# One modulation's weight sums moved from TensorE to VectorE, in a two-block network on one core

## The chip, the cores and the metric

The kernel runs on one core of a Trainium2 chip. The metric is the device time of one execution in microseconds, as the median of several runs. Engines are called as the profile calls them: PE is TensorE (PEld its weight loads), DVE is VectorE, ACT is ScalarE, POOL is GpSimd and SP is the queue that issues most DMAs.

## The reference, cut to what matters

The first block has two layers (`i`) of two sublayers (`j`) each: a mixer and a mixture of experts. Every sublayer is modulated by three rows of 1024 numbers that come from one vector `c`:

```python
def adaln_params(c, w, b):
    m = jax.nn.silu(c) @ w + b                      # c: 1024, w: 1024 x 3072
    shift, scale, gate = jnp.split(m, 3, axis=-1)
    return shift[:, None, :], scale[:, None, :], gate[:, None, :]
...
for i in range(DEPTH):
    shift, scale, gate = adaln_params(c, ada_w[i, 0], ada_b[i, 0])
    h = x * (1.0 + scale) + shift
    y = stick_breaking_attention(h, ...) if i == 0 else retention(h, ...)
    x = layer_norm(DEEPNORM_ALPHA * x + (1.0 + gate) * y, ...)
    shift, scale, gate = adaln_params(c, ada_w[i, 1], ada_b[i, 1])
    h = x * (1.0 + scale) + shift
    y = grouped_moe(h, ...)
    x = layer_norm(DEEPNORM_ALPHA * x + (1.0 + gate) * y, ...)
```

A second block (a state-space branch, sparse attention and a large table of experts) follows; the change does not touch it.

## The kernel before, in words

Everything is fp32 and 256 tokens long. `block1` runs the four sublayers in order. Work that belongs to a later sublayer is written as generators in `net.jobs`; `background` (L106) advances the first of them by one step, and the stages call it between their own pieces: after each projection of the first attention (L454 to L459), four times after each group of heads (L473, `ATR` = 4), and after each piece of the output projection (L435).

`ada_all` (L230) is such a generator: for one sublayer it makes the three rows shift, scale and gate by `ada_rows` (L206), and after the second it turns shift and scale into columns (`ada_cols`, L240). `ada_rows` loads its slice of the weight, 1024 x 1024, in four steps of 1 MB (L217; two blocks of 128 rows each), so a step brings two blocks of 128 x 1024. In each step PE multiplies: the stationary operand is silu(c) of the block, repeated in 32 columns (`crep`), the moving one 256 columns of the weight; four such products land in four strips of 32 partitions of one PSUM tile `y` of the pool `acc` (four tiles in all), which is held over the four steps. DVE then copies it out (L228, or L226 with the bias for the gate). A weight tile is taken from the pool `w` or, during the attention (`WIDE` = 2), mostly from the pool `hl`; each has six tiles. The profile records each of these fp32 products as two matmul instructions, so a step of eight products stands there as 16.

The order of the jobs (L1685) is: what is left of sublayer (0, 0)'s modulation, the small parameters of the second block's state-space branch, the modulation of (0, 1), and shift and scale of (1, 0). By the calls that `background` gets, the first three weight steps of (0, 1) come between the last projections of the attention, the other nine after the first three groups of heads, and those of (1, 0) after the third and fourth.

The first attention (`stick`, L438) makes q, k and v for four groups of four heads by projections whose weights are split into a rounded part (ACT, L151) and a rest (DVE, L153). Then, group by group, `stick_keep` (L482) multiplies q and k into PSUM (two tiles `ps`, of four, and one `y` per group), and DVE makes two passes over each (L499, L500) into tiles `t` of the pool `t4` (six of 128 x 1024) and `t2`; ACT takes Exp (L505) and Ln (L512); DVE adds (L513); PE sums over keys (L514 to L518), ACT takes Exp again (L519, L521), PE multiplies by v (L526, L529), and the result is split (L151, L153). A group's second half (`stick_mix`) is written behind the first half of the next group. After that come the output projection (`proj_out`, whose weights go through `w` and `hl` as well), the layer norm, the router and the experts (`moe`), which load 1 MB tiles into `w`, `hl` and `a`, 16 of them ahead.

The written order is not the issue order: the framework's scheduler plans each engine's queue when the kernel is built, and moves an instruction forward where its engine would otherwise have nothing. On the chip each queue then runs in its planned order.

Of the kernel before, what the change touches and what calls it, by code (L numbers as in the profile page):

```python
# [8 lines left out]
F32 = mybir.dt.float32  # L9
# [6 lines left out]
OP = mybir.AluOpType  # L16
# [3 lines left out]
P = 128  # L20
# [3 lines left out]
KB = 8  # L24
# [21 lines left out]
SCORE = 4.16  # L46
PACE = 2.81
PK = 128

# [3 lines left out]
class Net:  # L55
# [142 lines left out]

    def ada_init(self):
        nc = self.nc  # L200
        sc = self.cst.tile([P, KB], F32, name="c_silu")
        nc.scalar.activation(sc, self.c_col, AF.Silu)
        self.crep = self.cst.tile([P, KB, 32], F32, name="c_rep")
        nc.vector.tensor_copy(self.crep, sc[:, :, None].to_broadcast([P, KB, 32]))

    def ada_rows(self, i, j, slot, out):  # L206

        nc = self.nc
        W = self.io["ada_w"][i, j].rearrange("(k p) n -> p k n", p=P)
        if slot == 2:  # L210
            bias = self.wk.tile([P, 256], F32, name="ada_b", bufs=1)
            nc.gpsimd.dma_start(bias, self.io["ada_gate_b"][i * 2 + j])
        pm = self.acc.tile([P, 512], F32, name="y")[:, :256]
        for k2 in range(4):
            w = self.hl(F32) if self.wide > k2 % 3 else self.w()
            w = w.rearrange("p (k n) -> p k n", k=2)
            nc.sync.dma_start(w, W[:, k2 * 2:k2 * 2 + 2, slot * D:(slot + 1) * D])  # L217
            for k in range(2):
                kk = k2 * 2 + k
                for c in range(4):  # L220
                    self.mm(pm[32 * c:32 * c + 32], self.crep[:, kk, :],
                            w[:, k, c * 256:(c + 1) * 256], kk == 0, kk == 7)
            if k2 < 3:
                yield
        if slot == 2:
            nc.vector.tensor_tensor(out, pm, bias, op=OP.add)  # L226
        else:
            nc.vector.tensor_copy(out, pm)  # L228
# [1226 lines left out]
    def gates(self, t, eT):  # L1455
# [3 lines left out]
        if t == 0:  # L1459
            buf = self.tk.tile([P, 2048], F32, name="s", bufs=2)  # L1460
            self.tmp.append(buf[:, :512])
            self.hot = buf[:, 512:].bitcast(F16).rearrange("p (r j n q) -> p r j n q", r=2, n=PK, q=4)

        def hots(t4):

            o2, oh, ol = (self.hot[:, t4 // 4 % 2, j] for j in range(3))
            of = lambda j: eT[:, j, None, t4:t4 + 4].to_broadcast([P, PK, 4])
            V.tensor_tensor(ol, self.iota4, of(0), op=OP.is_equal)
# [5 lines left out]
        def fill(t4, o2, oh, ol):  # L1474
# [6 lines left out]
            if n:  # L1481
                V.tensor_tensor(sl[:, :, :n], pg[:, :, :n], sl[:, :, :n], op=OP.mult)
            if n < PK:
                nc.scalar.copy(sl[:, :, n:], pg[:, :, n:])
# [10 lines left out]
    def peer(self, hn, big, out):  # L1495
# [5 lines left out]
        self.phase("U")  # L1501
        for i in range(0, PK, 2):
            ps = self.psum((P, 2, S))
# [25 lines left out]
        nc.gpsimd.dma_start(h, self.h_dram)  # L1529
        for i in range(PK):  # L1530
            vr = self.up.tile([P, D], F32, name="raw")
# [5 lines left out]
            for t in range(T):  # L1537
                ts = slice(t * P, t * P + P)
                for hf in range(2):
                    cs = slice(hf * 512, hf * 512 + 512)  # L1540
                    self.mm3(y[t][hf], (ah[:, ts], al[:, ts]), (vp[:, 0, cs], vp[:, 1, cs]), i == 0, i == PK - 1)
        for t in range(T):
# [282 lines left out]
```

## Time and profile before

| | before |
|---|---|
| median of 3 runs | 2111.67 us (2110.96 to 2115.21) |
| profiled execution | 2115.24 us |
| its span in the trace | 2113.5 us |
| PE busy | 1995.0 us, 94% |
| DVE busy | 1229.3 us, 58% |
| ACT busy | 788.1 us, 37% |
| DMA | 496.13 MB, 235 GB/s on the mean |

Busy times are sums over the span and hide that the stages have different limits. Starts are microseconds from the start of the span; a row of the timeline merges neighbouring instructions of one kind. The end of a matmul is modelled, so the time that one takes from PE is read from start to start.

### The profile page before, as it was taken

To read this page: it belongs to the slowest core of one execution; us is meant where nothing else is said; L and a number is where in the kernel's file an instruction comes from. 1 tells how busy PE (TensorE), PEld (TensorE's weight loads), DVE (VectorE), ACT (ScalarE), POOL (GpSimd) and SP (SyncE) were. 2 spreads that over 40 slices of the span, in tenths; PEclk is the share of its full clock that TensorE was granted. 3 is DMA by queue.
4 is the path that set the end of the run, shared out by engine and by line. 5 is a ranking of instruction groups with operands and counts; after the bars stand their busy time and mean duration, and the time that the engine had idled before them with its cause. 6 is when DMAs were issued, how large, how long until landed. Compare 5 with 4: busy or idle time off the path is not lost.

```text
span 2113.5 us, 32410 instructions
## 1 busy us (share of the span) xinstructions
PE 1995.0 (94%) x12822; PEld 1564.7 (74%) x12823; DVE 1229.3 (58%) x2491; ACT 788.1 (37%) x1232; POOL 461.5 (22%) x351
## 2 busy tenths in 40 slices
PE   6999999989999999997876899999999999999998
PEld 4967545438888844445764789899999998888886
DVE  3554211137885411114698559876999886555555
ACT  3353111124454211113323444555444444444444
POOL 1002000002331200000354133544666550000000
PEclk8998999999999899998998999999999999999999
DMA  9797799995775799995322261444554445555554
GB/s 389 293 399 273 262 395 391 395 379 208 285 289 175 258 362 393 395 393 216 129 82 99 96 246 51 150 150 142 167 191 160 140 150 189 189 190 189 190 189 150
DMA packets 155603, 496.13 MB, mean 235 GB/s; under 512 B 10145, under 2 KB 10561, under 8 KB 146865
## 3 DMA queue, kind: packets, MB, share of 16 engines
q1 hardware_dynamic: 152592, 483.42, 63.6%
q0 software_dynamic: 2848, 10.53, 1.3%
q8 instruction: 104, 1.70, 0.3%
q14 instruction: 59, 0.48, 0.1%
HBM read 486.30 MB, written 7.61 MB: 234 GB/s over the span
## 4 chain that ended last, share of the span: by engine, by line
PE 52%; DVE 10%; issue 2%; ACT 1%; POOL 1%; POOLq 0%; ACTq 0%; DVEq 0%
PE ps L163 27%; PE y L163 23%; DVE t L1157 1%; DVE pair L1510 1%; DVE et L1434 1%; PE y L1163 1%; DVE i L1411 1%; DVE hl L153 1%; DVE t L1158 1%; POOL hl L160 0%; DVE pos L1422 0%; DVE t L1153 0%; DVE t L1152 0%; DVE v L1410 0%; DVE big L1518 0%
## 5 line engine op out<-in xcount | busy, mean ns | idle before, releaser
L163 PE MATMUL ps<-hn,pair 128*128 128x256 f32 x3072 | 383.4, 285 | 4.5 <-DVE pair L1510 4.3
L163 PEld LDWEIGHTS ps<-hn,pair 128*128 128x128 f32 x3072 | 373.8, 191 | 5.6 <-DVE pair L1510 5.1
L1510 POOL TENSOR_TENSOR pair<-raw,pair 128x640 fp32r<-128x640 f32 x128 | 235.4, 1846 | 160.1 <-ACT pair L1508 148.8
L163 PE MATMUL ps<-w,t 128*64 128x512 f32 x576 | 254.6, 595 | 5.4 <-DVE t L194 3.8
L163 PE MATMUL ps<-hl,t 128*64 128x512 f32 x576 | 254.2, 595 | 0.0
L151 ACT CAST hl<-w 128x2048 fp32r<-128x2048 f32 x79 | 150.1, 1902 | 137.7 <-PE ps L163 66.4
L153 DVE TENSOR_TENSOR pair<-raw,pair 128x1024 fp32r<-128x1024 f32 x128 | 156.9, 1226 | 67.2 <-ACT pair L151 67.2
L163 PE MATMUL y<-pair,tmp 128*128 128x512 f32 x768 | 189.5, 395 | 0.0
L163 PE MATMUL y<-pair,eT 128*128 128x512 f32 x768 | 186.3, 391 | 0.0
L163 PEld LDWEIGHTS y<-pair,tmp 128*128 128x128 f32 x768 | 144.4, 188 | 33.9
L163 PEld LDWEIGHTS ps<-w,t 128*64 128x64 f32 x576 | 76.3, 137 | 125.2 <-issue 117.4
L163 PEld LDWEIGHTS y<-pair,eT 128*128 128x128 f32 x768 | 144.1, 188 | 32.5
L1508 ACT CAST pair<-raw 128x1024 fp32r<-128x1024 f32 x128 | 134.1, 1051 | 66.9 <-PE ps L163 23.9
L153 DVE TENSOR_TENSOR hl<-w,hl 128x2048 fp32r<-128x2048 f32 x51 | 120.3, 2360 | 46.6 <-ACT hl L151 43.5
L330 POOL TENSOR_TENSOR ln_st<-ln_st,c_mhalf 128x1 f32<-128x1 f32 x8 | 6.3, 792 | 600.4 <-ACT ln_st L327 600.4
L151 ACT CAST pair<-raw 128x1024 fp32r<-128x1024 f32 x128 | 133.8, 1046 | 1.1 <-issue 1.1
L711 DVE TENSOR_TENSOR t<-t,ps 128x512 f32<-128x512 f32 x16 | 11.0, 688 | 210.8 <-PE ps L163 210.8
L163 PE MATMUL ps<-hl,a 128*128 128x256 f32 x1008 | 130.2, 287 | 1.8 <-ACT hl L151 1.8
L163 PEld LDWEIGHTS ps<-hl,a 128*128 128x128 f32 x1008 | 124.0, 191 | 6.1 <-ACT hl L151 2.0
L163 PE MATMUL ps<-a,hl 128*128 128x256 f32 x864 | 107.4, 285 | 2.5 <-DVE a L153 1.3
L163 PEld LDWEIGHTS ps<-a,hl 128*128 128x128 f32 x864 | 105.2, 193 | 5.2 <-DVE a L153 1.5
L163 PEld LDWEIGHTS ps<-hl,t 128*64 128x64 f32 x576 | 74.5, 137 | 37.6 <-issue 37.1
(424 smaller groups left out, 3126.7 us busy)
## 6 DMA issues: line engine op xcount, KB each, us to landing
raw<-peer_u SPq DMA_DIRECT2D x128, 512.0 KB, 3.5
raw<-peer_v SPq DMA_DIRECT2D x128, 512.0 KB, 3.4
w<-ada_w SPq DMA_DIRECT2D x35, 1024.0 KB, 9.4
w<-moe_w_gate SPq DMA_DIRECT2D x24, 1024.0 KB, 16.1
w<-moe_w_up SPq DMA_DIRECT2D x24, 1024.0 KB, 14.1
w<-moe_w_down SPq DMA_DIRECT2D x24, 1024.0 KB, 14.0
hl<-moe_w_gate SPq DMA_DIRECT2D x24, 1024.0 KB, 14.3
hl<-moe_w_up SPq DMA_DIRECT2D x24, 1024.0 KB, 14.1
```

Source lines behind the costliest of these rows:

```text
L151: nc.scalar.copy(hi, src)
L153: nc.vector.tensor_tensor(lo, src, hi.bitcast(F32), op=OP.subtract)
L163: self.nc.tensor.matmul(out, lhsT=lhsT, rhs=rhs, start=start, stop=stop, skip_group_check=True)
L330: nc.gpsimd.tensor_tensor(st[:, 3:4], st[:, 2:3], self.mhalf[:, 0:1], op=OP.pow)
L711: nc.vector.tensor_tensor(hid, hid, pu, op=OP.mult)
L1157: V.tensor_tensor_scan(w[:, ri], d, a[:, ri], 0.0, op0=OP.mult, op1=OP.add)
L1158: V.tensor_tensor(a, w, bc(c), op=OP.mult)
L1163: self.nc.tensor.matmul(py[32 * q:32 * q + 32, :S], lhsT=self.s5_ct[ct][:, 4 * i + q], rhs=ab[q % 2][:, x, ri], start=j == 0, stop=j == 3, ...
L1411: V.max_index(ix[:, a, rs], v[:, a, rs], s)
L1434: V.tensor_reduce(et[:, 0:2, h], oh.rearrange("p a k j -> p a j k"), axis=AX.X, op=OP.add)
L1508: nc.scalar.copy(up[:, 0], ur)
L1510: lo = eng.tensor_tensor(up[:, 1, ks], ur[:, ks], up[:, 0, ks].bitcast(F32), op=OP.subtract)
```

## The change

For the sublayers in `SUMS`, here (0, 1) alone, `ada_rows` takes no PSUM tile over its four steps. It takes a tile `t4` of 128 x 1024 instead, and DVE multiplies each block of the weight by silu(c), one number per partition, and adds it to that tile: one `tensor_scalar` for the first block of a row and seven `scalar_tensor_tensor` for the others. After the last block PE sums over the partitions with a stationary operand of ones (four products into the four strips of a `y`), and the copy follows as before. Loads, their tiles and the steps stay as they are.

```diff
+SUMS = ((0, 1),)
...
-        sc = self.cst.tile([P, KB], F32, name="c_silu")
+        sc = self.csilu = self.cst.tile([P, KB], F32, name="c_silu")
...
-        pm = self.acc.tile([P, 512], F32, name="y")[:, :256]
+        rows = (i, j) in SUMS
+        acc = self.t4() if rows else None
+        pm = None if rows else self.acc.tile([P, 512], F32, name="y")[:, :256]
         for k2 in range(4):
...
             for k in range(2):
                 kk = k2 * 2 + k
+                if rows:
+
+                    ck = self.csilu[:, kk:kk + 1]
+                    if kk == 0:
+                        nc.vector.tensor_scalar(acc, w[:, k], ck, None, op0=OP.mult)
+                    else:
+                        nc.vector.scalar_tensor_tensor(acc, w[:, k], ck, acc, op0=OP.mult, op1=OP.add)
+                    continue
                 for c in range(4):
                     self.mm(pm[32 * c:32 * c + 32], self.crep[:, kk, :],
                             w[:, k, c * 256:(c + 1) * 256], kk == 0, kk == 7)
             if k2 < 3:
                 yield
+        if rows:
+            pm = self.acc.tile([P, 512], F32, name="y")[:, :256]
+            for c in range(4):
+                self.mm(pm[32 * c:32 * c + 32], self.ones[:, :32], acc[:, c * 256:(c + 1) * 256], True, True)
         if slot == 2:
```

## Rows read from the trace of the kernel before

**Rows 1.** The page: the span and the busy time of each engine

```profile
span 2113.5 us, 32410 instructions
PE 1995.0 (94%) x12822; PEld 1564.7 (74%) x12823; DVE 1229.3 (58%) x2491; ACT 788.1 (37%) x1232; POOL 461.5 (22%) x351
```

**Rows 2.** Busy time by stretch; columns in the first line

```profile
core 0: us, PE busy (x) PEld busy (x) DVE busy (x) ACT busy (x) POOL busy (x), PEclk, DMA share, GB/s
60.00:80.00 20.00, 20.00 (x175) 19.28 (x174) 13.36 (x18) 9.11 (x11) 0.55 (x1) 1.00 0.84 319
80.00:97.00 17.00, 17.00 (x169) 15.60 (x167) 11.83 (x21) 7.37 (x8) 0.54 (x1) 1.00 0.52 165
97.00:114.00 17.00, 17.00 (x146) 16.91 (x143) 4.87 (x6) 2.28 (x6) 1.08 (x2) 1.00 1.02 407
114.00:172.00 58.00, 57.33 (x489) 34.53 (x487) 36.65 (x64) 33.13 (x44) 2.18 (x4) 1.00 0.96 368
172.00:193.00 21.00, 21.00 (x96) 17.32 (x93) 5.94 (x8) 2.90 (x4) 0.00 (x0) 1.00 0.44 167
193.00:224.00 31.00, 27.75 (x143) 25.62 (x142) 13.49 (x55) 7.45 (x14) 12.21 (x12) 0.61 0.70 262
...
163.60:172.10 8.50, 8.50 (x45) 5.66 (x44) 6.11 (x18) 5.19 (x9) 0.00 (x0) 1.00 0.95 360
260.00:300.00 40.00, 40.00 (x226) 20.79 (x224) 7.81 (x19) 5.73 (x13) 0.00 (x0) 1.00 1.04 392
```

**Rows 3.** Timeline of PE from 94 to 172 us: start, duration, what

```profile
94.24 2.80 PE L163 MATMUL y<-w,c_rep 128*32 128x256 f32 x48
...
120.74 1.07 PE L163 MATMUL y<-hl,c_rep 128*32 128x256 f32 x16
121.74 0.70 PE L163 MATMUL ps<-t,c_nones 128*128 128x256 f32 x2
...
126.97 1.98 PE L163 MATMUL ps<-t,c_pack 128*128 128x512 f32 x4
...
134.25 1.13 PE L163 MATMUL ps<-a 128*128 128x256 f32 x4
...
172.11 21.15 PE L163 MATMUL y<-hl,a 128*128 128x512 f32 x92
```

**Rows 4.** Busy time of the instructions that read `c_rep`, 94 to 172 us

```profile
94.00:172.00 78.00, 21.59 (x320) 9.51 (x320) 0.00 (x0) 1.00 0.97 371
```

**Rows 5.** DVE on L316 and L335: ns min/median/max, first and last start

```profile
L316 DVE SCALAR_TENSOR_TENSOR a<-x_mid,a x8: 1217/1225/1227, 191.3 to 976.8; 128x1024 f32<-128x1024 f32 x8
...
L335 DVE TENSOR_SCALAR a<-a,ln_st x6: 812/813/1751, 195.7 to 714.5; 128x1024 f32<-128x1024 f32 x6
```

**Rows 6.** Timeline of SP from 60 us: issue of the loads

```profile
80.81 15.84 SPq L217 DMA_DIRECT2D w<-ada_w  x5
...
104.32 22.29 SPq L217 DMA_DIRECT2D hl<-ada_w  x9
...
148.97 1.89 SPq L671 DMA_DIRECT2D w<-moe_w_gate  x2
...
197.98 2.64 SPq L671 DMA_DIRECT2D a<-moe_w_gate  x1
...
228.53 0.38 SPq L671 DMA_DIRECT2D w<-moe_w_up  x1
```

**Rows 7.** DMA issues from 60 to 224 us: count, KB, median us to landing

```profile
hl<-ada_w SPq DMA_DIRECT2D x13, 1024.0 KB, 10.5
w<-ada_w SPq DMA_DIRECT2D x7, 1024.0 KB, 5.8
...
a<-moe_w_gate SPq DMA_DIRECT2D x4, 1024.0 KB, 14.0
```

**Rows 8.** Timeline of DVE from 118 to 126 us, with idle time before

```profile
118.11 0.68 DVE L499 TENSOR_SCALAR t<-ps 128x512 f32<-128x512 f32 x1
...
123.86 1.23 DVE L513 TENSOR_TENSOR t<-t,t 128x1024 f32<-128x1024 f32 x1 [0.30 <-ACT t L512]
```

## The prediction

> **What bounds the kernel now.** I read the page first, then busy times by stretch, then the queues of PE, SP and DVE around the changed work. The page gives PE 94% of the span and DVE 58% [rows 1], but the change lives in one stage: the modulation of (0, 1) is summed between 94 and 144 us. There PE has no gap until 157 us: it is busy for all of 60 to 114 us and for 57.3 of the 58 us from 114 to 172, at the full granted clock [rows 2]. So the stage is bound by PE, with the modulation steps as filling between the products of the attention. DVE is at 36.7 of those 58 us, 63%, and the DMA engines are at 0.96 [rows 2]. The reader should see that PE is full because filling was always at hand, while the attention's chain (DVE passes, Exp and Ln on ACT, DVE add, PE, Exp, PE) runs beneath it.
>
> **What is removed.** A weight step is 16 matmul records on PE. One starts at 120.74 and the next work at 121.74, so it takes 1.00 us; three run in one row of 2.80 us, which is 0.93 each [rows 3]. All steps between 94 and 172 us are 320 records, 20 steps, in 21.59 us of busy time whose ends overlap [rows 4]; 12 of them are those of (0, 1), the other 8 stay. I take 1.00: PE loses 12.0 us, 3 steps ahead of 97 us and 9 after 120.
>
> **What is added on PE.** Per row, four products of the same shape, 8 records, half a step: 0.5 us, three times 1.5 us. No row shows them with a stationary operand of ones, but shape, type and strips are those of [rows 3]; at worst each of the 24 records takes as long as one of the two at 121.74 us, whose stationary operand is a constant too (0.63 us to the next start, 0.32 each [rows 3]): 7.6 us; at best they go at the pace of the 2.80 us row, 1.4. I take 1.5, the nearest shape. Net, **PE gives back 10.5 us** (4.4 to 10.6).
>
> **What is added on DVE.** Per row one `tensor_scalar` and seven `scalar_tensor_tensor` of 128 x 1024 fp32, SBUF to SBUF. Both forms are there: 1.225 us for the latter and 0.813 for the former at the median (1.751 at most, when something disturbs it) [rows 5]. Three rows: 21 x 1.225 + 3 x 0.813 = 28.2 us, up to 31.0. Each adds to the result of the one before it, so they run one after another.
>
> The first three steps of the shift row come with tiles `w`: the five loads from 80.81 us on land after 5.8 us at the median [rows 6, 7], and two earlier ones in the same pool lie before them. Their six sums, 6.9 us, find 6.6 us of idle DVE from 60 to 80, 5.2 from 80 to 97 and 12.1 from 97 to 114 [rows 2]. I cost them at nothing. Their cover is PE's projections, which wait for splits that DVE makes at the same time; without it a split is late by one sum, 1.2 us.
>
> The other nine steps are another matter. Their `hl` loads are issued from 104.32 us on, nine in 22.29 us, and land 10.5 us later [rows 6, 7]: from 114 us on, one every 2.5 us. Two sums take 2.45 us. From 114 us DVE gets 16 x 1.225 + 2 x 0.813 = 21.2 us on top of 36.65. The 8.5 us from 163.6 to 172.1 hold 6.11 us of DVE work [rows 2] that the attention does not need (the third split of the output projection, tables for a later sublayer, the columns of (1, 0)); it can slip behind. So DVE must do 36.65 - 6.11 + 21.2 = 51.7 us before the attention ends, not before 114 + 51.7 = 165.7 us.
>
> **The sum.** The attention ends for PE at 172.11 us, where the long row of the output projection begins [rows 3]. By PE alone it would end at 161.6; by DVE alone, without a gap, at 165.7. Some bubbles remain, since DVE waits for PE and ACT at a group's beginning; I allow the length of one DVE add, 1.2 us [rows 8], and take 167: **5 us earlier**. Bounds: 10.5 earlier where the sums of the gate row are all put off behind the attention (they are not needed for a long time), and later than before where they stand in its way (rivals).
>
> **The rest of the edit.** The copies (L226, L228) and columns stay, only their input comes later: 0. The tile `y` that a row held over its steps is free for the attention: at most a gain inside the bound. `acc` takes one of six `t4` tiles, of which two groups in flight use four: 0 while no third group needs two. Cover: the third group cannot start before PSUM of the first is free anyway. If it is gone, a group waits for the row's sum, one load pace of 2.5 us.
>
> **Queues.** The number and order of the loads stay. An `hl` tile is now freed by DVE after 2.45 us, not by PE after 1.00, and behind those loads SP holds the loads of (1, 0), the last ones of the output projection and the first expert weights at 148.97 us [rows 6]. Their cover: the 16 expert tiles loaded ahead are issued by 197.98 and land 14.0 us later, at 212 [rows 6, 7], while their first one is freed at 228.53 [rows 6]; 12 us or more. POOL's bias load and what is queued behind it (rows for the layer norm and positions) wait for the gate row's copy; they are used past 190 us, so nothing.
>
> **Does the gain pass on?** The output projection follows with PE full, 21.15 us [rows 3]; the layer norm and router come after. From 260 us the DMA engines are full at 392 GB/s [rows 2], so the experts are bound by loads, but the stream starts anew only as PE frees tiles, at 228.53 [rows 6]; it starts earlier by what the attention gains. I count it whole.
>
> **Standing of the number.** The profiled execution took 2115.24 us for a span of 2113.5, 1.7 around it; it lies 3.6 above the median of 2111.67. 2115.24 - 5 = 2110.2 for an execution like the profiled one, so 2106.7 for the median. A measurement tells about 0.2%, 4.2 us, from no change.
>
> **Rivals.**
> 1. *The sums take turns with the attention and the gain is used up.* Sums are written ahead of the second half of the first group; if the scheduler takes what is ready and written first, DVE does up to four steps, 9.8 us, before the add at 123.86 [rows 8], and PE has only 4 steps less to do meanwhile. PE then idles for what it saved. For: two sums need 2.45 us of every 2.5 us between landings [rows 5, 6]. Against: the plan moves work into gaps, and DVE has 21 us of them. Time: the attention ends within 2 us of before, 2110 to 2114 on the median.
> [...]
> 3. *The whole saving.* DVE puts the gate row behind the attention: 10.5 us, 2101.2. Against it: its `hl` tiles must be freed for the weights of the output projection.
> 4. *DVE does not sum.* Excluded: the edit names the engine, and forms and types are in [rows 5].
>
> **Chances.** Part of the saving (my forecast, 3 to 8 us faster) 0.36; rival 1 0.30; rival 2 0.24; rival 3 0.10. Of the first, 0.03 lies within 0.2%. Faster 0.43, same 0.33, slower 0.24. The forecast's own range is 2103 to 2109; to leave out no more than 2 in 10 the range takes in rival 3's end and the most of rival 2: 2101 to 2120.
>
> **What would show it.** Right: 128 records on `c_rep` in the stage instead of 320, and 24 new ones on the constant; 24 DVE instructions of 128x1024 with about 1.2 us each, mostly from 114 to 165 us with hardly a gap; PE with gaps of some 5 us in all there at clock 1.00; the long row of the output projection at about 167 us; the experts' loads earlier by the same. Wrong: DVE's sums longer than 1.3 us; the first group's add later than 128 us; a granted clock under 1.00 between 114 and 172; or that row at 172 or later.

## The result, and the profile after

The changed kernel took 2126.14 us (median of 6 runs, 2122.55 to 2128.88), the kernel before on the same chip 2111.32 us (6 runs): a ratio of 1.0069 with a 95% interval of 1.0056 to 1.0082. It is **slower by 14.8 us**; I had predicted 5 us faster, and the range ended at 2120.

The profiled execution took 2124.09 us with a span of 2121.2, only 8.9 more than the profiled one of before: that one lay 3.9 above its median, this one 2.1 below. For a fair comparison of rows I use a second profile of the kernel before, e1 below, with a span of 2109.2.

The page of the changed kernel: span, busy times, and the queue that it names "instruction" (packets, MB, share of the DMA engines).

```profile
span 2121.2 us, 32092 instructions
...
PE 1985.8 (94%) x12652; PEld 1559.9 (74%) x12655; DVE 1263.2 (60%) x2515; ACT 788.6 (37%) x1231; POOL 459.8 (22%) x351
...
q8 instruction: 102, 1.67, 0.3%
```

PE lost 9.2 us (10.5 predicted) and DVE gained 33.9 (28.2); yet the span grew. Such totals differ between two executions too: against e1 (PE 1990.2, DVE 1231.2) it is 4.4 and 32.0. Busy time by stretch, in the columns of [rows 2]:

```profile
80.00:97.00 17.00, 15.83 (x133) 15.44 (x131) 11.97 (x17) 7.67 (x9) 0.54 (x1) 1.00 0.48 145
97.00:114.00 17.00, 12.17 (x92) 12.20 (x93) 10.06 (x13) 1.13 (x3) 1.08 (x2) 0.80 1.00 400
114.00:140.00 26.00, 20.71 (x122) 14.81 (x122) 22.23 (x28) 11.66 (x16) 0.00 (x0) 0.87 0.89 349
140.00:172.00 32.00, 27.97 (x252) 16.91 (x247) 30.44 (x46) 16.93 (x20) 2.18 (x4) 1.00 0.88 304
...
114.00:179.50 65.50, 56.18 (x410) 36.82 (x408) 57.36 (x85) 33.67 (x45) 2.18 (x4) 0.95 0.90 330
```

PE was full from 60 to 157 us before. Now it is short by 4.8 us from 97 to 114, by 5.3 to 140 and by 4.0 to 172, and its granted clock falls to 0.80 and 0.87. DVE is busy for 30.4 of the last 32 us. Where PE stands still, and when the steps of [rows 3] come now (timeline of PE; the bracket is the idle time before, and what ended it):

```profile
95.45 0.38 PE L164 MATMUL y<-c_maskb,c_identb 128*128 128x512 bf16 x1
101.83 1.09 PE L188 MATMUL ps<-c_pack,t 128*128 128x128 f32 x4 [6.00 <-DVE t L1079]
102.57 12.66 PE L164 MATMUL ps<-a,hl 128*128 128x256 f32 x96
...
127.46 1.29 PE L164 MATMUL ps<-t,c_nones 128*128 128x256 f32 x4
134.04 3.78 PE L164 MATMUL ps<-t,c_pack 128*128 128x512 f32 x4 [5.29 <-DVE t L528]
...
140.38 0.92 PE L164 MATMUL ps<-a 128*128 128x256 f32 x3
...
179.56 20.70 PE L164 MATMUL y<-hl,a 128*128 128x512 f32 x90
```

The sums over keys come at 134.04 in place of 126.97, and take 3.78 us where the same shape took 1.98 [rows 3]: the granted clock from 134.04 to 137.82 is 0.50, and was 1.00 there before. The third group's products come at 140.38 (134.25), the long row of the output projection at 179.56 (172.11), so the attention ends 7.45 us later. The cause of both holes stands in DVE's queue. First hole and second hole in the timeline of DVE (L227 and L229 are the sums, L1079 makes small parameters of the second block, L154 a weight's rest, L528 is the add that was L513):

```profile
94.67 1.29 DVE L229 SCALAR_TENSOR_TENSOR t<-w,c_silu,t 128x1024 f32<-128x1024 f32 x1
...
97.08 1.16 DVE L229 SCALAR_TENSOR_TENSOR t<-w,c_silu,t 128x1024 f32<-128x1024 f32 x1
98.16 2.28 DVE L154 TENSOR_TENSOR hl<-w,hl 128x2048 fp32r<-128x2048 f32 x1
100.50 0.48 DVE L1090 MEMSET t<- 128x512 f32 x1
100.90 0.79 DVE L1079 TENSOR_TENSOR t<-t,t 64x256 f32<-64x256 f32 x2
...
129.12 1.27 DVE L229 SCALAR_TENSOR_TENSOR t<-hl,c_silu,t 128x1024 f32<-128x1024 f32 x1
130.31 0.68 DVE L515 SCALAR_TENSOR_TENSOR t<-t,ps 128x512 f32<-128x512 f32 x1
130.91 0.74 DVE L227 TENSOR_SCALAR t<-hl,c_silu 128x1024 f32<-128x1024 f32 x1
...
132.77 1.22 DVE L528 TENSOR_TENSOR t<-t,t 128x1024 f32<-128x1024 f32 x1
```

PE's queue holds four transposes of those small parameters; their input stands behind two sums and a split, and the attention's last projections stand behind them: 6.0 us. Before, the three weight steps at 94.24 [rows 3] lay in this place. The add of the first group starts at 132.77 in place of 123.86 [rows 8], behind three sums.

One more row I had not looked for: the conditional entry into the experts (a block for over-full experts is jumped over, once per layer). The instructions of that line, with ns min/median/max, in the changed kernel and in the kernel before:

```profile
L804 PEldq COMPARE_BRANCH  x2: 3422/3647/3872, 220.5 to 737.6; - x2
```

```profile
L789 PEldq COMPARE_BRANCH  x2: 416/430/445, 215.3 to 730.2; - x2
```

On PE the two branches take 7.3 us in place of 0.9; on the other engines they take under 0.1 us in both.

### The profile page after: what moved, and what is told of

Same layout as the page of the kernel before. It is cut to its first block, busy times and chain, and to the rows that moved or that the text cites. A ratio compares the mean times of both kernels' runs of the same rounds, so it can differ in the third digit from the quotient of the medians.

```text
span 2121.2 us, 32092 instructions
## 1 busy us (share of the span) xinstructions
PE 1985.8 (94%) x12652; PEld 1559.9 (74%) x12655; DVE 1263.2 (60%) x2515; ACT 788.6 (37%) x1231; POOL 459.8 (22%) x351
## 3 DMA queue, kind: packets, MB, share of 16 engines
q8 instruction: 102, 1.67, 0.3%
## 4 chain that ended last, share of the span: by engine, by line
PE 49%; DVE 13%; issue 2%; ACT 1%; POOL 0%; POOLq 0%; DVEq 0%; ACTq 0%
PE ps L164 26%; PE y L164 22%; DVE pair L1525 1%; DVE t L1172 1%; DVE i L1426 1%; DVE hl L154 1%; DVE et L1449 1%; DVE v L1425 1%; DVE pos L1437 1%; DVE cand L1432 1%; DVE t L1173 1%; DVE s L1428 0%; DVE t L1167 0%; DVE t L1168 0%; DVE big L1533 0%
## 5 line engine op out<-in xcount | busy, mean ns | idle before, releaser
L154 DVE TENSOR_TENSOR pair<-raw,pair 128x1024 fp32r<-128x1024 f32 x128 | 156.8, 1225 | 67.2 <-ACT pair L152 67.2
L164 PEld LDWEIGHTS y<-pair,tmp 128*128 128x128 f32 x768 | 144.4, 188 | 33.9
L154 DVE TENSOR_TENSOR hl<-w,hl 128x2048 fp32r<-128x2048 f32 x51 | 120.5, 2365 | 46.5 <-ACT hl L152 46.4
```

Of the source, the lines that this page charges most:

```text
L154: nc.vector.tensor_tensor(lo, src, hi.bitcast(F32), op=OP.subtract)
L164: self.nc.tensor.matmul(out, lhsT=lhsT, rhs=rhs, start=start, stop=stop, skip_group_check=True)
```

## The experiments

The theories: **Q**, the sums stand ahead of DVE work that PE waits for; **F**, PE has lost only its filling; **R**, later stages are planned anew by the scheduler and come out different; and, after the first four runs, **B**, the branch's price hangs on where PE's code lies. Times beside a ratio are medians; "before" is the kernel before, measured beside it on the same chip. The difference that a ratio gives can lie some us off that of the medians.

**e1: the kernel before once more** (an unused constant added).

> The kernel before with one unused constant added, for a second trace of it. Every theory: ratio 1.000 within 0.002. In its trace the long row of the output projection starts at 172 us within 1, and PE has no gap over 1 us from 40 to 157 us. What differs between this trace and the first one of before by several us elsewhere (first layer norm, entry of the second experts' block, the stage near 1160 us) is not an effect of the change.

2110.93 us, ratio 0.9985 (0.9975 to 0.9995). It has no hole of PE above 1 us in the attention, and its rows are those of before, shifted by 0.3 us. It ends 4.3 us ahead of the first profile of before, by differences of 1 to 3 us up to 860 us, none of them in the attention. So differences of 3 us between two profiles in those stretches say nothing. And though nothing was changed, the interval of the ratio leaves 1 out: a total within 0.2% of before, as in e2, e3, e5, e8, e11 and e12 below, says nothing by itself, and the readings rest on the traces.

**e2: sums as well as products.** The products stay, and DVE makes its 24 sums beside them.

```diff
+                if rows:
+                    ck = self.csilu[:, kk:kk + 1]
+                    ...
                 for c in range(4):
                     self.mm(pm[32 * c:32 * c + 32], self.crep[:, kk, :], ...)
```

> The kernel before with PE's products as they were, and DVE making the 24 sums too; what it sums is not used. Theory Q (DVE's queue: the sums stand ahead of DVE work that PE waits for): PE keeps its filling, yet the first group's add starts after 127 us instead of 123.9 and the attention ends 3 to 10 us later than before; time 3 to 12 us more. Theory F (PE's lost filling: holes and clock come from the products that went, whatever DVE does): within 2 us of before, no clock drop between 90 and 172 us. Theory R (the loss arises in later stages that were planned anew): attention within 2 us of before, time anywhere.

2116.14 us, 1.0016 (1.0003 to 1.0029). Timeline of PE around the two holes, and two stretches:

```profile
101.29 0.63 PE L188 MATMUL ps<-c_pack,t 128*128 128x128 f32 x4 [3.08 <-DVE t L1073]
...
132.05 1.98 PE L164 MATMUL ps<-t,c_pack 128*128 128x512 f32 x4 [1.34 <-DVE t L522]
```

```profile
114.00:140.00 26.00, 24.66 (x235) 16.70 (x233) 23.21 (x29) 12.28 (x17) 0.00 (x0) 1.00 0.94 364
140.00:172.00 32.00, 30.42 (x252) 18.06 (x252) 31.58 (x48) 18.14 (x22) 2.19 (x4) 1.00 0.89 315
```

The holes are shorter (3.08 and 1.34 us for 6.00 and 5.29), since products fill them, and the clock stays at 1.00 up to 193 us. Yet the branch into the experts comes at 221.1 us, against 214.0 in e1 and 220.5 in the changed kernel. The sums alone cost the attention a loss like that of the changed kernel, with PE's work unchanged and with no fall of the clock. So the loss needs neither a PE with less filling (F) nor a slower clock.

**e3: 63 of the 96 products left out** (three of the four strips, but for the first block), no sums; so part of the modulation is not computed.

```diff
-                for c in range(4):
+                few = (i, j) in SUMS
+                for c in range(1 if few and kk else 4):
```

> The kernel before with fewer products for sublayer (0, 1): of each row the first block's four products and one of four for the other seven blocks, 11 of 32, so 63 of 96 are left out and the modulation is not the reference's; no sums on DVE. That is 7.9 us of PE at 1.0 us for eight. Theory Q: DVE is not in the way, so the attention ends 5 to 8 us earlier and the time is 4 to 8 us less. Theory F: the holes and the clock drop appear as in the changed kernel, the attention ends no earlier than before, time 0 to 6 us more. Theory R: attention earlier, but time not less.

2110.11 us, 0.9988 (0.9974 to 1.0002). This run tells nothing of the theories, because the edit did not take PE's time away. Timeline of PE, the same three steps as the first row of [rows 3]:

```profile
95.31 2.78 PE L164 MATMUL y<-w,c_rep 128*32 128x256 f32 x18
```

18 records took 2.78 us, as 48 did in 2.80 [rows 3]: a block with one product in one strip took as long here as a block with four in four strips. e7 asks the question again.

**e4: the shift row back on PE**; scale and gate stay on DVE.

```diff
-        rows = (i, j) in SUMS
+        rows = (i, j) in SUMS and slot > 0
```

> The changed kernel with the shift row of (0, 1) back on PE, scale and gate still summed on DVE (16 sums). Theory Q: the 6.0 us hole of PE at 95.8 us, where it waits for the small state-space parameters on DVE, is gone, so the last projections start at 98.5 us as before and not at 102.6; the second hole before the first group's add stays at 3 us or more. Attention 2 to 4 us later than before, time 2 to 9 us more than before and 4 to 8 less than the changed kernel. Theory F: the first hole shrinks by the filling alone, 2.7 us. Theory R: time as the changed kernel, 13 to 16 us over before.

2118.69 us, 1.0026 (1.0016 to 1.0036). Timeline of PE, and the stretches behind it:

```profile
98.01 0.60 PE L188 MATMUL ps<-c_pack,t 128*128 128x128 f32 x4
...
126.44 2.53 PE L164 MATMUL ps<-t,c_pack 128*128 128x512 f32 x4 [2.71 <-DVE t L528]
...
178.72 21.15 PE L164 MATMUL y<-hl,a 128*128 128x512 f32 x92
```

```profile
114.00:140.00 26.00, 22.44 (x105) 13.90 (x105) 22.60 (x28) 13.28 (x18) 0.00 (x0) 0.80 1.02 400
140.00:172.00 32.00, 27.68 (x234) 15.91 (x233) 27.18 (x42) 16.09 (x19) 2.18 (x4) 0.84 0.74 256
```

The first hole is gone with the sums that stood there, as Q says, and the sums over keys are back at 126.4. But the attention's end is not back: the long row comes at 178.72. The first hole explains that the projections started 4.0 us late in the changed kernel (102.57 for 98.53 before), and next to nothing of the lateness at 179. DVE is less full here than in the changed kernel (53.4 of the 64.7 us from 114 to 178.7), and the clock is lower in the second stretch: e4 doesn't tell which of the two keeps the end late. Its branches took 3317 and 328 ns: one of them was slow and one was not, with the same sums ahead of both.

**e5: the changed kernel with its code moved.** Twenty small products at the start, where PE waits for its first weights.

```diff
         consts1(net)
+        pt = net.psum()
+        for _ in range(20):
+            net.mm(pt[:32, :16], net.ones[:, :32], net.ones[:, :16], True, True)
```

> The changed kernel with 20 small products (32 by 16, ones by ones) put on PE's queue at the start, while PE still waits for its first weights (11.6 us), so that all later code of PE lies 80 instructions further on; nothing else differs. The two branches into the experts took PE 3422 and 3872 ns in the changed kernel and 445 and 416 ns in the kernel before. [...] Rival (the branch waits for something that the sums delay, a transfer or another engine): both branches still 3.3 to 3.9 us, total about 2126 us.

2114.94 us, 1.0015 (1.0002 to 1.0029). The branches took 445 and 1063 ns, for 3422 and 3872 in the changed kernel. The attention has its two holes (6.00 and 5.28 us) and its late end as before. Theory B's sign holds, and the gain is larger than the 5.8 us of the branches (11.2 us below the first measurement of the changed kernel, which was made apart); e9 and e10 repeat it side by side.

**e6: the kernel before with its code moved**, by eleven such products.

> The kernel before with 11 such small products at the start: PE's later code lies 44 instructions further on, no sum is on VectorE. Theory B: both branches cost 3 to 4 us, the attention is as before (long row of the output projection at 172), total about 2111.3 + 6.4 = 2117.7 us (2116 to 2120). Rival (the sums delay what the branch waits for): both branches 0.3 to 0.5 us, total 2110 to 2113 us.

2120.29 us, 1.0032 (1.0017 to 1.0048): **no sum on DVE, no change to the attention, and 9.2 us slower by the medians** (6.8 by the ratio). The traces show the same order of instructions in both on DVE, ACT and POOL (2491, 1232 and 351), so the schedule did not change with it. The first branch took 3917 ns, as expected; the second 409, which was not expected. But a few instructions behind the second branch, timeline of PE, and then the same place in e1:

```profile
733.85 0.30 PE L187 MATMUL ps<-c_pack,t 128*128 128x128 f32 x1
735.85 5.73 PE L163 MATMUL ps<-t,a 128*128 128x128 f32 x28 [1.70 <-issue]
```

```profile
727.91 5.02 PE L164 MATMUL ps<-t,a 128*128 128x128 f32 x28
```

In e1 these 28 matmuls follow without a gap. "issue" is time in which PE waits for nothing that the profile shows. So the price of a moved code seems to show either in the branch or just behind it; no run ties this gap to the code's place by itself.

**e7: narrow products.** 84 of the 96 products take 16 columns in place of 256; the rest of those sums is left out, and no sum is on DVE. All 96 stay, so PE's code does not move but for two instructions.

```diff
+                    n = 16 if (i, j) in SUMS and kk else 256
-                    self.mm(pm[32 * c:32 * c + 32], self.crep[:, kk, :],
-                            w[:, k, c * 256:(c + 1) * 256], kk == 0, kk == 7)
+                    self.mm(pm[32 * c:32 * c + 32, :n], self.crep[:, kk, :],
+                            w[:, k, c * 256:c * 256 + n], kk == 0, kk == 7)
```

> The kernel before in which 84 of the 96 products of the second sublayer's modulation take 16 columns in place of 256 (the rest of those sums is left out); the number of instructions and their order stay, no sum is on VectorE. So PE loses about 10 us of work between 94 and 163 us and VectorE gains none. The prediction's step (PE bounds the stage and gives back what it loses): 2100 to 2103 us. Theory Q (VectorE's queue holds PE up in the changed kernel): no hole of PE above 1.5 us at 95 to 102, first group's add on VectorE at 122 to 125, granted clock 1.00 in 97 to 140, total 2104 to 2111 us. Theory F (PE had only lost its filling): holes of some us at the same places as in the changed kernel, granted clock under 0.9 in 97 to 114 or in 114 to 140, total 2110 to 2118 us.

2099.70 us, 0.9940 (0.9919 to 0.9961). PE by stretch:

```profile
97.00:114.00 17.00, 17.00 (x144) 16.98 (x143) 5.52 (x8) 3.51 (x8) 1.08 (x2) 1.00 1.02 406
114.00:140.00 26.00, 24.90 (x264) 16.43 (x263) 16.03 (x30) 14.09 (x20) 0.00 (x0) 1.00 1.02 408
140.00:172.00 32.00, 32.00 (x263) 20.09 (x257) 20.58 (x34) 19.09 (x25) 2.18 (x4) 1.00 0.90 340
```

With 10 us of PE's work gone and nothing put on DVE, there is no hole above 1.1 us and no fall of the clock up to 172 us; the branch comes at 206.9, 7.1 us ahead of e1 (and its start was 1.0 later). F falls: a PE with less filling does not get holes by itself. Of the 11.4 us of the median, those 7.1 are there at the branch, with the attention behind; most of the rest is R (below, at e12), less a slow second branch of 3259 ns.

**e8: the sums later.** The changed kernel with the third sublayer's two rows ahead of the second sublayer's modulation, and the twenty small products.

```diff
-        net.jobs += [...] + [ada[0, 1], without_gate((1, 0))]
+        net.jobs += [...] + [without_gate((1, 0)), ada[0, 1]]
```

> The changed kernel (all three rows summed on VectorE, and the 20 small products of e5 at the start) with two entries of the list of jobs exchanged: the third sublayer's two rows (on PE) come before the second sublayer's modulation, so the sums start after the second group of the attention's adds in place of at 89 us. Theory Q: the transposes of the small state-space parameters run at 97 to 99 and the first group's add at 122 to 126, with no hole of PE above 2 us before 130; what is lost is only what the sums delay after 140; long row of the output projection at 170 to 176, total 2108 to 2115 us. Rival (VectorE's total work bounds the attention wherever the sums stand): long row at 178 to 181, total 2117 to 2122 us.

2114.81 us, 1.0010 (0.9997 to 1.0023). Timeline of PE, and the stretches:

```profile
99.39 0.60 PE L188 MATMUL ps<-c_pack,t 128*128 128x128 f32 x4
...
128.19 1.98 PE L164 MATMUL ps<-t,c_pack 128*128 128x512 f32 x4
```

```profile
114.00:140.00 26.00, 26.00 (x198) 17.26 (x197) 19.06 (x29) 14.62 (x20) 0.00 (x0) 1.00 1.02 409
140.00:172.00 32.00, 22.40 (x91) 11.75 (x90) 32.00 (x39) 16.57 (x20) 1.08 (x2) 0.81 0.60 212
```

Both holes are gone, and up to 140 us PE is full at full clock: Q was right about the holes. Then DVE is busy for all 32.00 of 32 us and PE for 22.4, and the branch comes at 221.0, as late as in every kernel with all the sums. The rival was right about the end: **DVE's work sets it here, though the sums stand elsewhere** (DVE is busy for all of 140 to 178.5 us, and the output projection's row follows at 178.52). The total time hides this, because the later stages gave some back.

**e9 and e10: the changed kernel, and the changed kernel with 21 small products**, on one chip.

> The changed kernel once more, as the partner on the same chip of the next run. Theory B: branches of PE into the experts 3.3 to 3.9 us each as in its first profile; total 2121 to 2127 us. Rival (the first measurement of the changed kernel was set apart by its chip or its launches): 2113 to 2118 us with the same rows. In both, PE's holes at 96 to 102 and at 129 to 134 stand again.

> The changed kernel with 21 small products at the start (one more than in e5, where the second branch still took 1063 ns in place of 416): PE's later code lies 84 instructions further on. Theory B: both branches 0.3 to 0.5 us, the attention as in e9; total below e9's by the price of the second branch alone (3.1 us between 726 and 851, the first being swallowed by the experts' transfers) or of both (6.4 us): 2115 to 2121 us. Rival (branches don't set the time): within 1.5 us of e9.

e9 took 2124.28 us, 1.0059 (1.0045 to 1.0073); e10 2116.41, 1.0025 (1.0013 to 1.0036). The branches, e9 and then e10:

```profile
L805 PEldq COMPARE_BRANCH  x2: 3622/3677/3732, 221.5 to 738.7; - x2
```

```profile
L804 PEldq COMPARE_BRANCH  x2: 445/644/843, 221.8 to 735.3; - x2
```

So 84 instructions of dead work, at a time when PE has nothing else to do (from 2.41 us on; its next matmul waits for a load until 11.07), take 7.9 us off the changed kernel. The order of the instructions on DVE, ACT and POOL (2515, 1231 and 351) is the same in both traces, so it is not a new schedule. The branches are 6.1 us shorter by their own durations, but the first one's 3.2 have no effect left at 430 us (table below); the second one's 2.9 stand, and where the rest comes from is not shown.

**e11: the gate row alone on DVE, late**, behind the third sublayer's rows, with 29 small products; and **e12: the same order of jobs with all products on PE.**

```diff
-        net.jobs += [...] + [ada[0, 1], without_gate((1, 0))]
+        net.jobs += [...] + [without_gate((0, 1)), without_gate((1, 0)), ada[0, 1]]
```

> Only the gate row of the second sublayer's modulation is summed on VectorE (8 operations, 9.4 us), the scale and shift rows stay on PE, and the job that makes the gate row is moved behind the third sublayer's two rows, so its sums start after the add of the third group, near 150 us; 29 small products at the start. Theory Q: VectorE no longer holds PE up before 150 (no hole of PE above 2 us there), PE loses 4.0 - 0.5 = 3.5 us, the branch into the experts comes 1 to 4 us earlier than in e12, total 2102 to 2108 us if the later stage's hole of 6.7 us shrinks to 2.2 us as in all replanned kernels so far, else 2107 to 2112. Rival (sums take turns with the last groups and the output projection wherever they stand): branch 1 to 5 us later than in e12, total 2108 to 2114 us.

> The kernel before with the same order of jobs as e11 (the gate row's products moved behind the third sublayer's rows, all on PE): no sum on VectorE. Theory R (part of what the changed kernel gains comes from the later stages being planned anew, whatever the edit): the branch into the experts at 213 to 216 as before, PE's hole of 6.7 us near 1160 falls to 2.2 us, total 2105 to 2109 us. Rival (that hole shrank because of the sums): it stays at 6.7 us, total 2110 to 2113 us.

e11 took 2111.50 us, 0.9994 (0.9981 to 1.0007), e12 2109.00, 0.9988 (0.9978 to 0.9998). In e11 the branch comes at 212.8, in e12 at 216.5: with 8 sums in place of 24 DVE has room, and of the 3.7 us some 2.8 are left when the 0.9 is taken off by which e11 is ahead at 65 us: most of PE's relief of 3.5. But e11 gives 2.2 of it back by 248 us (a gap of 2.37 us for "issue" at 218 us, a few instructions behind its branch) and 2.5 more from 430 to 726 us. e12 is ahead of the kernel before by its interval, but by less than 0.2%, as e1 was.

R shows in the second block, far from the edit. Timeline of PE in the kernel before, and at the same place in the changed one (what was L1158 is L1173 there) and in e7:

```profile
1165.71 1.06 PE L1163 MATMUL y<-t,c_s5m 128*32 128x256 f32 x2 [6.68 <-DVE t L1158]
```

```profile
1177.02 0.44 PE L188 MATMUL y<-c_pack,t 128*128 128x128 f32 x2 [2.17 <-DVE t L1258]
```

```profile
1158.42 0.44 PE L188 MATMUL y<-c_pack,t 128*128 128x128 f32 x2 [2.17 <-DVE t L1245]
```

The hole is 6.66 to 6.68 us in before, e1 and e6, where the jobs of the attention were left alone, and 2.2 to 2.7 us at this place in all others, e3, e7 and e12 without a sum among them. The traces show the new plan itself. From the branch into the first experts on, DVE has 2234 instructions, and in e1 and e6 their order is that of before; in the changed kernel 330 places of this order hold another instruction, and in e7, without a sum, all but 2 places are as in the changed kernel. So each edit here that touched the attention's jobs was planned anew far behind them, and gained some 4 to 6 us at this place.

## Why the prediction was wrong

How late one instruction is against the same instruction of e1, at nine places (start in the kernel less start in e1, us; the first column is the time in e1):

```
  e1     before  changed    e9    e10     e2     e7     e8     e6
   65      0.3     0.7     1.7    0.2    0.2    1.0    1.5    1.8
  214      1.4     6.6     7.6    7.8    7.1   -7.1    7.0    2.9
  430      1.3     6.4     7.9    7.7    6.8   -7.3    5.8    4.2
  726      4.4    11.8    12.8    9.5   10.5   -6.2    6.4    6.1
  851      4.6    14.9    16.0    7.6   10.2   -3.4    9.5    8.4
 1153      4.2    15.9    17.0    8.7   11.0   -2.7    9.8    9.2
 1173      4.2     9.5    10.5    2.3    4.6   -9.1    4.1    9.3
 1354      4.3     9.7    10.8    2.5    4.9   -8.8    5.9    9.3
 2090      4.3    12.0    14.1    1.2    4.9   -9.0    5.5   13.2
```

The columns are single executions: e9's was its slowest and e10's its fastest, so they end 12.9 us apart where the medians are 7.9 apart; e6's lay 3.8 above its median. Three causes stand in the table. The attention with the norm and the router behind it (65 to 214): +5.5 to +7.6 for the kernels with all the sums on DVE, with PE's relief (changed, e9, e10, e8) and without it (e2); -8.1 for the relief without sums (e7). The place of PE's code: +3 from 726 to 851 in the changed kernel, e9, e7 and e8, the four with a slow second branch, and +2 in e6, with the gap behind its branch. The new plan: 4 to 6 us back from 1153 to 1354. For the changed kernel against e1: 0.7 at 65 us, then 5.9 in the attention, -0.2 to 430, 5.4 to 726, 3.1 to 851, 1.0 to 1153, -6.2 to 1354 and 2.3 behind it make 12.0. Its first branch's 3.4 us cost nothing net by 430 us. From 1354 to 2090 the changed kernel, e9 and e6 lose 2.3 to 3.9, the others nothing. Between 1360 and 1770 us PE waits for DVE's tiles `pair` for 3.5 us in the changed kernel, 3.3 in e9, 2.9 in e6, 2.2 in e1 and 0.9 in e10; what lengthens these waits is open.

By the steps of the prediction:

- *What is removed and added.* Right. 320 records on `c_rep` became 128, and there are 24 new ones on the constant. Busy time of the instructions that read `c_rep`, then `c_ones`, 94 to 172 us; then the sums, ns min/median/max:

```profile
94.00:172.00 78.00, 7.91 (x128) 4.16 (x128) 0.91 0.90 333
...
94.00:172.00 78.00, 1.92 (x24) 0.47 (x24) 0.00 (x0) 0.91 0.90 333
```

```profile
L229 DVE SCALAR_TENSOR_TENSOR t<-hl,c_silu,t x12: 1271/1276/1285, 117.1 to 154.1; 128x1024 f32<-128x1024 f32 x12
...
L227 DVE TENSOR_SCALAR t<-hl,c_silu x2: 745/746/746, 123.3 to 130.9; 128x1024 f32<-128x1024 f32 x2
```

  The sums take 1.276 and 0.746 us for the 1.225 and 0.813 that I used.
- *PE gives back 10.5 us.* Right in kind, where nothing is put on DVE: e7 gives 8.1 of about 10. And the step "does the gain pass on": it did in e7, from -7.1 at the branch to -7.3 at 430 us.
- *"It can slip behind", and bubbles of 1.2 us.* **This is the step that failed.** I let DVE do 51.7 us before the attention ends. The row of 114 to 179.5 us above shows 57.4: the 6.1 us that could have slipped did not; splits, tables and columns ran between 160 and 179 us. And 8.1 of these 65.5 us are idle (3.8 to 140, 1.6 to 172, 2.8 behind it) where I allowed 1.2. 51.7 + 6.1 + 1.2 would already end at 173.0, later than the 172.11 of before; the 57.4 and the 8.1 idle that were measured end at 179.5. e8, with no hole before 140 us and DVE at 32.00 of 32, shows that DVE bounds the end there; e2 fits, with 56.8 of 64.6 us and PE's clock at 1.00. So DVE took PE's place as the bound. In the changed kernel and e4 DVE also waits, and how much of that the slower clock makes is not shown. The page's 58% for DVE [rows 1] and the 63% of the stage [rows 2] did not tell me that 21 us more leave no slack when DVE and PE wait for each other in turns.
- *The first three steps' sums cost nothing.* Wrong at its place: a hole of 6.0 us, projections 4.0 us later, a clock of 0.80 in that stretch. I had named the cover as PE's projections that wait for splits; the work that waited was another, the transposes for the second block, which a job list put into PE's queue. It did not decide the end: from 65 to 214 us e4, without it, loses 5.5 us on e1, and the changed kernel 5.9.
- *Rival 2*, slower by a fallen clock, came true by the marks: the add at 132.77 (later than 128), a granted clock under 1.00 (0.87 from 114 to 140 us), and slower. No run shows the price of a fallen clock that the range's upper end of 2120 rests on. In its place the runs show this: in the changed kernel the granted clock was 0.50 from 134.04 to 137.82, and the sums over keys took 3.78 us there in place of 1.98; in e2 the clock stays at 1.00 up to 193 us, and the attention ends as late, so a fallen clock is not needed for the loss. By stretch the clock was 0.80 with a hole of 6.0 us and 0.87 with 5.29; in e4 it was 0.80 with one of 2.71, and in e2, with 3.08 and 1.34, it stayed at 1.00. What the fall cost by itself no run shows.
- *What I left out.* That removing 84 products moves all later code of PE by 336 instructions (two matmuls and two weight loads each in the built programs; the pages have 170 PE and 168 PEld records less), and that a plan made anew differs in stages which the change does not touch. The first costs 7.9 us between e9 and e10, the second gives 4 to 6.

So of the 14.8 us about 6 are the attention. The code's place is worth 7.9 by e9 against e10, of which the rows place about 3, at the second branch. Against these stands the new plan's gain of 6. A loss of 5.4 us from 430 to 726 us was not followed: it is between 0.6 and 5.4 us in all kernels of the table, and 3.1 between two profiles of the kernel before. It and the 2.3 us from 1354 on may be part of the code's price; that is not shown.

## What to carry to other kernels

Moving work to an engine with idle time needs that engine's whole queue up to the stage's end: take all that is planned there, without leaving out what could be put off, and leave room for the waits between the engines. Here 58 us of DVE's work for a stretch of 58 us lost, since 8 us of idle time came on top; a third of the sums, put late (e11), left room and gained some 2.8 us at the same place. Test the two halves apart (relief alone, load alone), since here they were -8 and +7 us, and both together +5.5 to +7.6. And before a difference under half a per cent is put down to an edit, move the code by some dead instructions and look for stages that were planned anew: here these two were worth 8 and 6 us, in an effect of 15.

## What the runs showed of the hardware

How far PE's code ahead of the first and of the second branch lies from its place in the kernel before, in instructions (counted in the built programs, two loads and two matmuls for an fp32 product; PE's records in the traces give the same within 3), and what PE's two branches took:

```
kernel            moved      first branch, ns   second branch, ns
before, e1, e2        0            445                416
changed, e9        -337, -336  3422, 3622         3872, 3732
e4                 -224           3317                328
e3                 -252            445                416
e5                 -257, -256      445               1063
e6                  +44           3917                409
e7                   -2, -1        445               3259
e8                 -258            445               3810
e10                -253, -252      445                843
e11                  +5            352                415
e12                  +1            445               1083
```

In these runs a branch took 328 to 1083 ns or 3259 to 3917 and nothing between, and it turned within one or two instructions (the second branch, 3259 ns in e7 and 416 before). The first is slow at -337, -224 and +44; near 0 it took 352 to 445 ns, and from -252 to -258 again 445. The second is slow at -336, -258 and -1, and fast from -256 to -252 (1063, 843 and 416 ns), at -224 and +44 (328 and 409) and from 0 to +5 (415 to 1083). A slow branch took about 2.8 to 3.5 us more than the same branch in the kernel before. What lies behind this pattern no run shows. The page above has 102 packets, 1.67 MB, on the queue "instruction"; that PE waits for one of them at a slow branch no row shows.

A second thing: in e3 a strip of 32 columns used alone took as long as four used together (2.78 us for 18 records, 2.80 for 48 in the kernel before), so leaving out 30 of those 48 records saved PE 0.02 us there.
